# Reading v, k and q of one accumulator bank on ScalarE first, with VectorE's low halves behind

## The chip, the core and the metric

The kernel runs on one core of a Trainium2 chip. A core has TensorE (PE, matmuls; its weight loads are shown as PEld), VectorE (DVE), ScalarE (ACT), GpSimd (POOL) and SyncE (SP, which here issues nearly all DMAs). Each engine works through its own list of instructions in order, and engines wait for each other by semaphores. Matmul results land in PSUM, which has eight banks; ACT and DVE read them from there. The metric is the device time of one execution in microseconds; lower is better.

## The reference

One layer of a streaming encoder with two token mixers side by side: differential attention ("A", 4 heads of two rotated 64-wide queries and keys) and stick-breaking attention ("B", 8 heads, no rotation). There are 2048 prompt rows, and 8 x 16 sample rows with a cache of 512 keys each. Cut to what matters here:

```python
qa, ka, va, za, qb, kb, vb, zb, ga, gb = split(h @ w_in)
qa, ka = rope(qa, pos), rope(ka, pos)
# A
w = softmax(s1) - lam * softmax(s2);  oa = w @ va
# B: no rotation
z = qb @ kb.T * 64 ** -0.5;  mask = kpos < qpos
log_1m = where(mask, log_sigmoid(-z), 0)
log_a = log_sigmoid(z) + reverse_cumsum(log_1m) - log_1m
ob = where(mask, exp(log_a), 0) @ vb
y = (sigmoid(ga) * ya + sigmoid(gb) * yb) @ w_out
```

The new keys and values of both mixers are outputs as well.

## The kernel before

**Units and tiles.** The work of the mixers is cut into eight units, two heads' worth of 128 columns each; units 0, 2, 4 and 6 are of kind 0 (A) and 1, 3, 5 and 7 of kind 1 (B). Each unit goes over 17 row tiles of 128 rows, the sample tile first. A tile has a projection (`project`): 24 matmuls of 128 x 512 into one bank named ps_mm (L467), giving q, k, v and the gate input z, 128 columns each. Two banks serve ps_mm in turn. Beside it run 24 matmuls of the output gates (L543, bank ps_t). Six transposes (L561, L565) turn q and k, and copies (L575, L576) bring them to SBUF.

**Precision by halves.** Matmuls run in float16, so every operand is a pair: a high half, rounded to float16, and a low half, the remainder. ScalarE makes the high half (`S.activation`, L318 within `split`, and L501 for the query, which it writes twice), VectorE the low half (`V.scalar_tensor_tensor`, L323 and L502), which reads the same source and subtracts the high half.

**Leaving the bank.** `finish`, at the projection's last matmul, empties the bank. For kind 1: ACT copies k and v (pr, L485) and z (L489) out in float32, then come `halves(vt)`, `halves(k16)` and `query`, each a high half on ACT and then its low half on DVE. All of them read the one bank. For kind 0 the bank is read for pr (L481) and v only; q and k come from the rotated rows in SBUF that POOL makes (L508 to L513).

**Scores of B.** For each head and 512 keys: two matmuls and a mask into a bank ps_s (L708, L709, L712; three banks), two sigmoids on ACT (L134), a scan on DVE (L682). At the end of up to 1024 keys POOL multiplies (L688), ACT casts the high half (L616), DVE makes the low half (L619), and SP issues a transposing DMA (L626) whose result feeds the value matmuls (L769, L770; L765 to L767 for A).

**What sets the order.** The program is written as interleaved streams: scores of a tile, pieces of projections some 5 tiles ahead (`take`, `position`, `LEAD`), weights' preparation at the side. From that the framework's scheduler builds each engine's list by its own model of time and puts in the semaphores. Two engines never get the same PSUM bank at once: it orders their accesses, reads among themselves too. So the list of every engine can change around an edit. Projections reload their rows (hs, three tiles, L444) by DMA; a tile's hs is free when its projection and its gates are done.

Of the kernel before, what the change touches and what calls it, by code (L numbers as in the profile page):

```python
# [21 lines left out]
AF = mybir.ActivationFunctionType  # L22
ALU = mybir.AluOpType
# [3 lines left out]
P = 128  # L27
# [97 lines left out]
def layer_kernel(ctx: ExitStack, tc: tile.TileContext, a: dict):  # L125
    nc = tc.nc
    V, S, G, T = nc.vector, nc.scalar, nc.gpsimd, nc.tensor
# [12 lines left out]
    def kept(x):  # L140
        tc.keep_in_program_order(x)
        return x
# [37 lines left out]
    def out_rows(name, t, lo, n):  # L180
        p, s = outs[name]
        return p[t * P : (t + 1) * P, lo : lo + n] if t < NT else s[:, lo : lo + n]
# [28 lines left out]
    def bank(tag, dt=F32):  # L211
        return ps.tile([P, 512 if dt == F32 else 1024], dt, tag=tag, name=f"ps_{tag}", bufs=BANKS[tag])
# [102 lines left out]
    def split(hi, lo, src, s, on=None):  # L315

        if on is S:
            S.activation(out=hi, in_=src, func=AF.Identity, scale=s)  # L318
        elif on is G:
            G.tensor_scalar(out=hi, in0=src, scalar1=s, scalar2=0.0, op0=ALU.mult, op1=ALU.add)  # L320
        else:
            V.tensor_scalar(out=hi, in0=src, scalar1=s, scalar2=None, op0=ALU.mult)
        V.scalar_tensor_tensor(out=lo, in0=src, scalar=s, in1=hi, op0=ALU.mult, op1=ALU.subtract)  # L323
# [114 lines left out]
    def late(u, t):  # L438
        return u == 7 and NT - LATE <= t < NT

    def fetch_h(u, t):
        ahead[u, t] = hs[len(fetched) % 3].bitcast(F16).rearrange("p (f k n) -> p f k n", f=2, n=P)
        fetched.append(t)
        load(out=ahead[u, t], in_=hT_d[t // 4][:, t % 4, :, :, :])  # L444

    def project(U, t):

        kind, h, sc, sq = U["kind"], U["h"], U["sc"], U["sq"]
        g, i = t // 4, t % 4
        box = {}  # L450

        def start():
            if t in at_hand:
                box["h"] = at_hand.pop(t)
            else:
                if (U["u"], t) not in ahead:
                    fetch_h(U["u"], t)
                box["h"] = ahead.pop((U["u"], t))
            box["p"] = bank("mm")
            if kind == 0:  # L460
                box["r"] = stg.tile([P, 96], F32, tag="rope", name="rope")
                load(out=box["r"], in_=a["shapes"][:, t * 96 : t * 96 + 96])

        def mm(n):
            hi, wi = ((0, 0), (0, 1), (1, 0))[n % 3]
            k = n // 3
            T.matmul(box["p"], box["h"][:, hi, k, :], U["w"][k][:, wi, :], start=(n == 0), stop=(n == 3 * KT - 1))  # L467

        def piece(n):
            if n == 0:  # L470
                start()
            for j in range(2 * n, 2 * n + 2):
                mm(j)
            if n == 11:
                finish()

        def finish():
            p, s2, s = box["p"], sc[:, 2:3], sq[:, 0:1]
            pr = stg.tile([P, 512], F32, tag="pr", name="pr", bufs=3)
            if kind == 0:  # L480
                S.activation(out=pr, in_=p, func=AF.Identity, scale=sc[:, 1:2])  # L481
            elif t == NT:
                S.activation(out=pr[:, P:512], in_=p[:, P:512], func=AF.Identity, scale=sc[:, 1:2])
            else:
                S.activation(out=pr[:, P:384], in_=p[:, P:384], func=AF.Identity, scale=sc[:, 1:2])  # L485

                assert t % len(rings) not in silu_z
                silu_z[t % len(rings)] = rings[t % len(rings)]
                S.activation(out=rings[t % len(rings)], in_=p[:, 384:512], func=AF.Identity, scale=sc[:, 1:2])  # L489

            qb = qbuf[t % len(qbuf)]
            k16 = stg.tile([P, 2, 2, 64], F16, tag="k16", name="k16")
            vt = kvp.tile([P, 2, 2, 64], F16, tag="v", name="v", bufs=V_BUFS)

            def halves(dst, src, scale):
                src = src.rearrange("p (c d) -> p c d", d=64)
                split(dst[:, :, 0, :], dst[:, :, 1, :], src, scale, S)

            def query(src, scale):
                src = src.rearrange("p (c d) -> p c d", d=64)  # L500
                S.activation(out=qb[:, 0, :, :, :], in_=src.unsqueeze(2).to_broadcast([P, 2, 2, 64]), func=AF.Identity, scale=scale)  # L501
                V.scalar_tensor_tensor(out=qb[:, 1, :, 0, :], in0=src, scalar=scale, in1=qb[:, 0, :, 0, :], op0=ALU.mult, op1=ALU.subtract)  # L502
            if kind == 0:
                cosT, sinT = box["r"][:, 0:32], box["r"][:, 32:96]
                x4 = pr[:, 0:256].rearrange("p (c f d) -> p c f d", c=4, f=2)
                rot = stg.tile([P, 256], F32, tag="rot", name="rot")
                r2 = stg.tile([P, 256], F32, tag="r2", name="r2", bufs=1)
                G.tensor_tensor(out=rot.rearrange("p (c f d) -> p c f d", c=4, f=2), in0=x4,  # L508
                                in1=cosT.unsqueeze(1).unsqueeze(1).to_broadcast([P, 4, 2, 32]), op=ALU.mult)
                G.tensor_tensor(out=r2.rearrange("p (c f d) -> p c f d", c=4, f=2), in0=x4[:, :, ::-1, :],  # L510
                                in1=sinT.rearrange("p (f d) -> p f d", f=2).unsqueeze(1).to_broadcast([P, 4, 2, 32]),
                                op=ALU.mult)
                G.tensor_tensor(out=rot, in0=rot, in1=r2, op=ALU.add)  # L513
                halves(vt, p[:, 256:384], s2)
                query(rot[:, 0:128], s)
                halves(k16, rot[:, 128:256], s)
            else:
                rot = pr
                halves(vt, p[:, 256:384], s2)
                halves(k16, p[:, 128:256], s2)  # L520
                query(p[:, 0:128], s2)
            nk, nv = ("ak", "av") if kind == 0 else ("bk", "bv")
            load(out=out_rows(nk, t, h * P, P), in_=rot[:, 128:256])
            load(out=out_rows(nv, t, h * P, P), in_=pr[:, 256:384])
            ui = (h + 4 * kind) * P
            if kind == 0 or t == NT:
                load(out=z_d[t][:, ui : ui + P], in_=pr[:, 384:512])
            U["v"][t] = vt
            if t == NT:
                load(out=s_d[U["u"]][:, 6:8, :], in_=vt.rearrange("p c f d -> p c (f d)"))  # L530
            U["q16", t], U["k16", t] = qb, k16

        g0, gw = GATES[U["u"]]
        per = 1024 // gw if gw else 0

        def gate_piece(n):

            if n == 0:
                box["g"] = bank("t")
            for j in range(per * n, per * n + per):  # L540
                hi, wi = ((0, 0), (0, 1), (1, 0))[j % 3]
                k = j // 3
                x = T.matmul(box["g"][:, 0:gw], box["h"][:, hi, k, :], U["wg"][k // per][:, k % per, wi, :], start=(j == 0), stop=(j == 3 * KT - 1))  # L543
# [916 lines left out]
    with ExitStack() as c2:  # L1460
        def pool2(name, bufs):
            return c2.enter_context(tc.tile_pool(name=name, bufs=bufs, reuse_waits="tile"))
# [3 lines left out]
        s2 = pool2("s2", 2)  # L1466
# [169 lines left out]
```

## Time and profile before

| | us |
|---|---|
| timed runs | 2216.34, 2220.72, 2229.65 |
| median | 2220.72 |
| profiled execution | 2225.32 |
| its span, first to last instruction | 2223.5 |
| TensorE busy in the span | 2061.2 |
| VectorE busy | 1743.8 |
| ScalarE busy | 1606.2 |

The span falls into a start of some 120 us, then the units one after the other, A and B in turn up to about 1760 us, and the merge of the branches with the sample's attention behind that. An engine's idle time is put down to the instruction that released it; such a row gives total, number of waits and the longest. Idle time of an engine that isn't the slowest costs nothing by itself.

### The profile page before, as it was taken

What the parts mean: (1) busy time and instruction counts of PE and PEld (TensorE: products, weight loads), DVE (VectorE), ACT (ScalarE), POOL (GpSimd) and SP (SyncE); (2) the same over time, 40 slices, a digit from 0 to 9 for tenths busy, and PEclk for the clock granted to TensorE, in tenths of its full rate; (3) what the DMA queues carried; (4) which work ended last, traced back from release to release, by engine and by line L of the source; (5) the groups of instructions that cost most, each with busy time, mean ns of one, the idle gap of its engine ahead of it and who ended that gap; (6) DMA issues with size and microseconds to landing.
All of it is one profiled execution on the core that took longest, in us unless ns stands there. A gap on an engine that the chain in (4) does not pass through costs nothing. (4 is left out here: it accounts for less than half of the span.)

```text
span 2223.5 us, 41495 instructions
## 1 busy us (share of the span) xinstructions
PE 2061.2 (93%) x14608; PEld 1110.4 (50%) x14608; DVE 1743.8 (78%) x3799; ACT 1606.2 (72%) x3212; POOL 699.6 (31%) x608
## 2 busy tenths in 40 slices
PE   5999999999999999999999998989998788899997
PEld 3655555555555455555554554555454444444443
DVE  4667869789887788988778888777789877787864
ACT  3978677789877677978677788876688666666531
POOL 1232014356410443742024355301334412111210
PEclk8999999999999999999999999999999899999999
DMA  9778559899796889979879999985787999999762
GB/s 323 258 241 201 120 139 217 181 227 203 200 252 158 222 201 202 207 205 221 198 195 216 191 224 207 241 181 130 159 170 155 201 280 255 230 254 224 194 166 67
DMA packets 824978, 451.05 MB, mean 203 GB/s; under 512 B 556122, under 2 KB 763274, under 8 KB 824256
## 3 DMA queue, kind: packets, MB, share of 16 engines
q1 hardware_dynamic: 823820, 448.01, 82.7%
q8 instruction: 114, 1.87, 0.3%
q14 instruction: 96, 0.79, 0.1%
q10 hardware_dynamic: 948, 0.39, 0.1%
HBM read 229.87 MB, written 86.02 MB: 142 GB/s over the span
## 5 line engine op out<-in xcount | busy, mean ns | idle before, releaser
L688 POOL TENSOR_TENSOR sc_p<-sc_p,sc_n 128x127 f32<-128x127 f32 (+7 forms) x192 | 313.3, 1635 | 663.1 <-DVE sc_n L682 510.6
L467 PEld LDWEIGHTS <-hs 128*128 128x128 f16 x3120 | 293.3, 99 | 318.5 <-issue 6.4
L467 PE MATMUL ps_mm<-wa,hs 128*128 128x512 f16 x1590 | 391.2, 382 | 5.3 <-DMA hs<-hT_d 5.0
L467 PE MATMUL ps_mm<-wb,hs 128*128 128x512 f16 x1530 | 377.4, 380 | 0.0
L682 DVE TENSOR_TENSOR_SCAN sc_n<-ps_s,sc_n,zero_t 128x512 f32<-128x512 f32 x192 | 245.4, 1278 | 33.3 <-ACT ps_s L134 28.1
L708 PE MATMUL ps_s<-k,qst 128*128 128x512 f16 (+3 forms) x640 | 223.2, 350 | 30.0 <-DVE sc_n L682 22.8
L543 PEld LDWEIGHTS <-hs 128*128 128x128 f16 x1632 | 155.0, 98 | 181.7 <-DVE qst L576 5.1
L543 PE MATMUL ps_t<-wa,hs 128*128 128x512 f16 x1020 | 242.3, 380 | 2.1 <-DVE qst L576 2.0
L619 DVE TENSOR_TENSOR sc_n<-sc_p,sc_n 128x128 f16<-128x128 f32 (+7 forms) x192 | 217.7, 1137 | 32.9 <-ACT sc_n L616 32.3
L134 ACT ACTIVATE sc_p<-ps_s,usc 128x512 f32<-128x512 f32 (+3 forms) x320 | 203.9, 637 | 34.4 <-PE ps_s L709 23.0
L709 PE MATMUL ps_s<-k,qst 128*128 128x512 f16 (+3 forms) x640 | 223.6, 350 | 0.0
L616 ACT CAST sc_n<-sc_p 128x128 f16<-128x128 f32 (+7 forms) x192 | 155.0, 809 | 57.3 <-POOL sc_p L688 55.8
L134 ACT ACTIVATE ps_s<-ps_s,usc 128x512 f32<-128x512 f32 (+3 forms) x320 | 196.3, 613 | 0.0
L543 PE MATMUL ps_t<-wb,hs 128*128 128x512 f16 x612 | 151.7, 383 | 4.8 <-DMA hs<-hT_d 2.1
L769 PE MATMUL ps_o<-v,wt 128*128 128x128 f16 x1088 | 135.2, 224 | 22.1 <-DMA wt<-sc_n 21.9
L1535 PE MATMUL ps_o<-wo,wb 128*128 128x512 f16 x624 | 141.6, 382 | 1.1 <-ACT wb L1309 1.1
L602 DVE TENSOR_SCALAR_CACHE_REDUCE sc_p<-ps_s,usc 128x512 f32<-128x512 f32 (+3 forms) x160 | 106.2, 664 | 35.7 <-PE ps_s L709 20.5
L770 PE MATMUL ps_o<-v,wt 128*128 128x64 f16 x1088 | 127.1, 196 | 0.0
L769 PEld LDWEIGHTS <-wt 128*128 128x128 f16 x1088 | 101.0, 100 | 50.1 <-DMA wt<-sc_n 25.3
L682 DVE TENSOR_TENSOR_SCAN sc_n<-ps_s,zero_t 128x128 f32<-128x128 f32 (+3 forms) x128 | 104.0, 813 | 27.7 <-ACT ps_s L134 27.7
L1501 PEld LDWEIGHTS <-wa 128*128 128x128 f16 x816 | 77.7, 98 | 94.2 <-issue 4.1
L1544 POOL TENSOR_TENSOR x<-m,x 128x512 f32<-128x512 f32 x32 | 45.6, 1427 | 247.1 <-DVE m L1539 138.7
(378 smaller groups left out, 4548.6 us busy)
## 6 DMA issues: line engine op xcount, KB each, us to landing
hs<-hT_d SPq DMA_DIRECT2D x132, 512.0 KB
g_d<-gt SPq DMA_DIRECT2D x68, 256.0 KB
out_dram<-pr SPq DMA_DIRECT2D x204, 64.0 KB
o_d<-o SPq DMA_DIRECT2D x136, 64.0 KB
wa<-g_d SPq DMA_DIRECT2D x17, 512.0 KB
wb<-g_d SPq DMA_DIRECT2D x17, 512.0 KB
hs<-o_d SPq DMA_DIRECT2D x17, 512.0 KB
wide<-in_w_ada_dram SPq DMA_DIRECT2D x8, 1024.0 KB
```

The source lines that it names most:

```text
L134: i = S.activation(**kw)
L467: T.matmul(box["p"], box["h"][:, hi, k, :], U["w"][k][:, wi, :], start=(n == 0), stop=(n == 3 * KT - 1))
L543: x = T.matmul(box["g"][:, 0:gw], box["h"][:, hi, k, :], U["wg"][k // per][:, k % per, wi, :], start=(j == 0), stop=(j == 3 * KT - 1))
L616: x = S.copy(out=hi, in_=src)
L619: V.tensor_tensor(out=lo, in0=src, in1=hi, op=ALU.subtract)
L682: V.tensor_tensor_scan(out=dst[:, lo : lo + n][:, ::-1], data0=src[:, 0:n][:, ::-1], data1=zero_t[:, 0:1].to_broadcast([P, n]), initial=fi ...
L688: G.tensor_tensor(out=p[:, 0:m], in0=p[:, 0:m], in1=n[:, 1 : m + 1], op=ALU.mult)
L708: T.matmul(p[:, 0:n], qst[:, c, :], kk[:, c, 0:n], start=True, stop=False)
L709: T.matmul(p[:, 0:n], qst[:, 2 + c, :], kk[:, c, 0:n], start=False, stop=not diag)
L769: T.matmul(po[:, c * P : (c + 1) * P], wt[:, wj, :], vt[:, c, :, :], start=first, stop=False)
L770: T.matmul(po[:, c * P : c * P + 64], wt[:, nb + wj, :], vt[:, c, 0, :], start=False, stop=last)
L1535: T.matmul(po, st["y"][:, yi * 8 + k, :], wo[j * 4 + k // 2][:, wi, k % 2, :], start=(n == 0), stop=(n == 3 * KT - 1))
```

## The change

For kind 1 the three high halves are read first, then the three low halves follow. For kind 0 the order of the six instructions is what it was; the helpers are only split in two.

```diff
-            def halves(dst, src, scale):
-                src = src.rearrange("p (c d) -> p c d", d=64)
-                split(dst[:, :, 0, :], dst[:, :, 1, :], src, scale, S)
-
-            def query(src, scale):
-                ...
+            def parts(src):
+                return src.rearrange("p (c d) -> p c d", d=64)
+
+            def high(dst, src, scale):
+                S.activation(out=dst[:, :, 0, :], in_=parts(src), func=AF.Identity, scale=scale)
+
+            def low(dst, src, scale):
+                V.scalar_tensor_tensor(out=dst[:, :, 1, :], in0=parts(src), scalar=scale, in1=dst[:, :, 0, :], op0=ALU.mult, op1=ALU.subtract)
+
+            def query_high(src, scale):
+                S.activation(out=qb[:, 0, :, :, :], in_=parts(src).unsqueeze(2).to_broadcast([P, 2, 2, 64]), func=AF.Identity, scale=scale)
+
+            def query_low(src, scale):
+                V.scalar_tensor_tensor(out=qb[:, 1, :, 0, :], in0=parts(src), scalar=scale, in1=qb[:, 0, :, 0, :], op0=ALU.mult, op1=ALU.subtract)
...
             else:
                 rot = pr
-                halves(vt, p[:, 256:384], s2)
-                halves(k16, p[:, 128:256], s2)
-                query(p[:, 0:128], s2)
+                high(vt, p[:, 256:384], s2)
+                high(k16, p[:, 128:256], s2)
+                query_high(p[:, 0:128], s2)
+                low(vt, p[:, 256:384], s2)
+                low(k16, p[:, 128:256], s2)
+                query_low(p[:, 0:128], s2)
```

The number of instructions on each engine stays the same; lines behind L520 move by 12 (L616 is now L628, L682 is L694, L619 is L631, L749 is L761). On ACT, at the projection of tile 10 of unit 3, the list was this (pr, szs, v, k_10278 and qbuf are what the bank is read into, sc_p and sc_n the scores of B, ob an output of the value matmuls):

```order
L485 ACTIVATE pr<-ps_mm,usc_8232 128x256
L489 ACTIVATE szs<-ps_mm,usc_8232 128x128
L318 ACTIVATE v<-ps_mm,usc_8232 128x2x64
L134 ACTIVATE sc_p<-ps_s,usc_8232 128x512
L134 ACTIVATE ps_s<-ps_s,usc_8232 128x512
L134 ACTIVATE r_10317<-szs 128x128
L616 CAST sc_n<-sc_p 128x1024
L749 ACTIVATE ob<-ps_o,usc_8232 128x128
L318 ACTIVATE k_10278<-ps_mm,usc_8232 128x2x64
L616 CAST sc_n<-sc_p 128x128
```

There k stands six places behind v, and q (L501) four places behind k. At the same projection ACT's list with the change is:

```order
L134 ACTIVATE sc_p<-ps_s,usc_8232 128x512
L134 ACTIVATE ps_s<-ps_s,usc_8232 128x512
L134 ACTIVATE r_10317<-szs 128x128
L485 ACTIVATE pr<-ps_mm,usc_8232 128x256
L489 ACTIVATE szs<-ps_mm,usc_8232 128x128
L499 ACTIVATE v<-ps_mm,usc_8232 128x2x64
L499 ACTIVATE k_10278<-ps_mm,usc_8232 128x2x64
L505 ACTIVATE qbuf_213<-ps_mm,usc_8232 128x256
L761 ACTIVATE ob<-ps_o,usc_8232 128x128
L628 CAST sc_n<-sc_p 128x128
```

The five reads of the bank stand in one piece, and two sigmoids and the silu's sigmoid now stand ahead of it. On DVE, the low halves of the same projection stood here before (k and qst are the copies of the turned keys and queries, o an output of B):

```order
L576 COPY qst<-ps_t 128x512
L323 SCALAR_TENSOR_TENSOR v<-ps_mm,usc_8232,v 128x2x64
L682 SCALAR_TENSOR_TENSOR sc_n<-ps_s,sc_n,zero_t 128x512
L732 TENSOR_TENSOR szs<-szs,r_10317 128x128
L619 TENSOR_TENSOR sc_n<-sc_p,sc_n 128x1024
L750 SCALAR_TENSOR_TENSOR o<-ps_o,usc_8232,ob 128x128
L323 SCALAR_TENSOR_TENSOR k_10278<-ps_mm,usc_8232,k_10278 128x2x64
L619 TENSOR_TENSOR sc_n<-sc_p,sc_n 128x128
L682 SCALAR_TENSOR_TENSOR sc_n<-ps_s,zero_t 128x256
L502 SCALAR_TENSOR_TENSOR qbuf_213<-ps_mm,usc_8232,qbuf_213 128x2x64
```

With scans and other low halves between them, v, k and q lie nine places apart. DVE's list at this projection with the change is:

```order
L588 COPY qst<-ps_t 128x512
L694 SCALAR_TENSOR_TENSOR sc_n<-ps_s,sc_n,zero_t 128x512
L744 TENSOR_TENSOR szs<-szs,r_10317 128x128
L502 SCALAR_TENSOR_TENSOR v<-ps_mm,usc_8232,v 128x2x64
L502 SCALAR_TENSOR_TENSOR k_10278<-ps_mm,usc_8232,k_10278 128x2x64
L508 SCALAR_TENSOR_TENSOR qbuf_213<-ps_mm,usc_8232,qbuf_213 128x2x64
L762 SCALAR_TENSOR_TENSOR o<-ps_o,usc_8232,ob 128x128
L631 TENSOR_TENSOR sc_n<-sc_p,sc_n 128x128
L631 TENSOR_TENSOR sc_n<-sc_p,sc_n 128x1024
L694 SCALAR_TENSOR_TENSOR sc_n<-ps_s,zero_t 128x256
```

The three low halves stand together behind a scan, and the scan of 256 columns comes behind them.

More of the change, by code (lines that the diff above doesn't have):

```diff
@@ L493, in finish @@
             vt = kvp.tile([P, 2, 2, 64], F16, tag="v", name="v", bufs=V_BUFS)
-            def halves(dst, src, scale):
-                src = src.rearrange("p (c d) -> p c d", d=64)
-                split(dst[:, :, 0, :], dst[:, :, 1, :], src, scale, S)
-            def query(src, scale):
-                src = src.rearrange("p (c d) -> p c d", d=64)
-                S.activation(out=qb[:, 0, :, :, :], in_=src.unsqueeze(2).to_broadcast([P, 2, 2, 64]), func=AF.Identity, scale=scale)
-                V.scalar_tensor_tensor(out=qb[:, 1, :, 0, :], in0=src, scalar=scale, in1=qb[:, 0, :, 0, :], op0=ALU.mult, op1=ALU.subtract)
+            def parts(src):
[8 more added lines that the diff above has]
+                V.scalar_tensor_tensor(out=qb[:, 1, :, 0, :], in0=parts(src), scalar=scale, in1=qb[:, 0, :, 0, :], op0=ALU.mult, op1=ALU.subtract)
             if kind == 0:
@@ L513, in finish @@
                 G.tensor_tensor(out=rot, in0=rot, in1=r2, op=ALU.add)
-                halves(vt, p[:, 256:384], s2)
-                query(rot[:, 0:128], s)
-                halves(k16, rot[:, 128:256], s)
+                high(vt, p[:, 256:384], s2)
+                low(vt, p[:, 256:384], s2)
+                query_high(rot[:, 0:128], s)
+                query_low(rot[:, 0:128], s)
+                high(k16, rot[:, 128:256], s)
+                low(k16, rot[:, 128:256], s)
             else:
                 rot = pr
-                halves(vt, p[:, 256:384], s2)
-                halves(k16, p[:, 128:256], s2)
-                query(p[:, 0:128], s2)
+                high(vt, p[:, 256:384], s2)
+                high(k16, p[:, 128:256], s2)
+                query_high(p[:, 0:128], s2)
+                low(vt, p[:, 256:384], s2)
+                low(k16, p[:, 128:256], s2)
+                query_low(p[:, 0:128], s2)
             nk, nv = ("ak", "av") if kind == 0 else ("bk", "bv")
```

## The prediction

> **What bounds the kernel now.** I read the page first, then busy time by stretch, then the groups of the instructions that the change touches, then the waits. The page gives the span and the shares.
>
> ```profile
> span 2223.5 us, 41495 instructions
> PE 2061.2 (93%) x14608; PEld 1110.4 (50%) x14608; DVE 1743.8 (78%) x3799; ACT 1606.2 (72%) x3212; POOL 699.6 (31%) x608
> ```
>
> The profiled execution took 2225.32 us, of which the span is 2223.5 and 1.8 lies around it; the three timed runs have the median 2220.72. I work differences out in the trace and take them off the median.
>
> TensorE is busy 93% of the time. The change acts only where projections of stick-breaking units run, which is four stretches, since projections run some tiles ahead of the scores that use them. The columns are stretch, length, then busy time of PE, PEld, DVE, ACT and POOL, the granted clock, the DMA share and GB/s:
>
> ```profile
> 215.00:420.00 205.00, 197.41 (x1386) 107.78 (x1384) 163.90 (x361) 150.54 (x331) 46.72 (x44) 0.99 0.69 162
> 660.00:860.00 200.00, 191.83 (x1324) 103.49 (x1323) 156.76 (x312) 149.21 (x314) 60.01 (x53) 1.00 0.82 196
> 1090.00:1290.00 200.00, 192.13 (x1323) 103.12 (x1322) 158.30 (x296) 152.23 (x320) 68.14 (x58) 1.00 0.85 194
> 1500.00:1700.00 200.00, 187.84 (x1341) 102.36 (x1339) 158.33 (x294) 144.88 (x304) 62.91 (x51) 0.97 0.71 155
> ```
>
> TensorE is idle 7.6, 8.2, 7.9 and 12.2 us there, 35.8 us in 805. That is all that a better order of ACT and DVE could win in these stretches while TensorE's own work is unchanged.
>
> One place looks different, the end of the last unit:
>
> ```profile
> 1670.00:1680.00 10.00, 9.75 (x88) 5.64 (x86) 9.74 (x15) 10.00 (x22) 3.76 (x4) 1.00 0.68 156
> 1690.00:1700.00 10.00, 6.83 (x37) 3.75 (x37) 9.89 (x13) 6.26 (x12) 4.77 (x3) 0.57 0.74 145
> 1700.00:1710.00 10.00, 7.19 (x63) 3.97 (x61) 9.89 (x10) 7.94 (x13) 4.92 (x4) 1.00 0.61 119
> ```
>
> Here DVE is busy 9.7 to 9.9 us of every 10 while TensorE falls to 7: VectorE's scans set the pace, and what arrives late at DVE is lost.
>
> **The change, part by part.** It removes waits of ScalarE and adds no instruction. The groups concerned (busy, mean ns | idle before, and what ended it):
>
> ```profile
> L318 ACT ACTIVATE k<-ps_mm,usc 128x128 f16<-128x128 f32 x68 | 25.7, 378 | 24.6 <-DVE v L323 24.2 <-PE ps_t L561 0.2
> L501 ACT ACTIVATE qbuf<-ps_mm,usc 128x256 f16<-128x256 f32 x68 | 32.2, 474 | 41.9 <-DVE k L323 41.9
> L323 DVE SCALAR_TENSOR_TENSOR v<-ps_mm,usc,v 128x128 f16<-128x128 f32 x136 | 46.6, 342 | 16.0 <-ACT v L318 15.2
> L323 DVE SCALAR_TENSOR_TENSOR k<-ps_mm,usc,k 128x128 f16<-128x128 f32 x68 | 22.8, 336 | 1.5 <-ACT k L318 1.5
> L502 DVE SCALAR_TENSOR_TENSOR qbuf<-ps_mm,usc,qbuf 128x128 f16<-128x128 f32 x68 | 23.2, 341 | 13.6 <-ACT qbuf L501 13.2
> ```
>
> ACT stands 24.2 + 41.9 = 66.1 us, about 1 us for each of the 68 projections, until DVE has finished a low half, although k's and q's high halves need nothing from it: the two engines take turns on the bank. DVE stands 1.5 + 13.2 = 14.7 us for k and q, and up to 15.2 us for v (rotated units share that row). All of this is replaced by one hand-over per projection.
>
> What one projection looks like (unit 3, tile 10, that of the order rows shown above):
>
> ```profile
> 802.30 0.52 ACT L485 ACTIVATE pr<-ps_mm,usc 128x256 f32<-128x256 f32 x1
> 802.65 0.42 ACT L489 ACTIVATE szs<-ps_mm,usc 128x128 f32<-128x128 f32 x1
> 802.90 0.42 ACT L318 ACTIVATE v<-ps_mm,usc 128x128 f16<-128x128 f32 x1
> 804.84 0.34 DVE L323 SCALAR_TENSOR_TENSOR v<-ps_mm,usc,v 128x128 f16<-128x128 f32 x1
> 805.85 0.36 ACT L318 ACTIVATE k<-ps_mm,usc 128x128 f16<-128x128 f32 x1
> 806.10 0.29 ACT L616 CAST sc_n<-sc_p 128x128 f16<-128x128 f32 x1
> 807.87 0.34 DVE L323 SCALAR_TENSOR_TENSOR k<-ps_mm,usc,k 128x128 f16<-128x128 f32 x1
> 808.24 0.47 ACT L501 ACTIVATE qbuf<-ps_mm,usc 128x256 f16<-128x256 f32 x1 [0.24 <-DVE k L323]
> 810.22 0.32 DVE L502 SCALAR_TENSOR_TENSOR qbuf<-ps_mm,usc,qbuf 128x128 f16<-128x128 f32 x1
> ```
>
> The bank is read from 802.30 to 810.54, 8.2 us, because each turn also queues behind whatever its engine has in order. With the reads together, ACT's five starts lie 0.35, 0.25, 0.25 and 0.25 apart (802.30 to 802.65 to 802.90, and 805.85 to 806.10 for a read of 128 columns), and q takes 0.47: 1.6 us in one piece. Three lows follow, each start some 0.26 behind the other, 0.9 us. The bank could be free after 2.5 us instead of 8.2.
>
> Does anyone need it earlier? Hardly. TensorE's waits near it in the whole span (total, times, longest):
>
> ```profile
> PE ps_mm L467 <- DVE v L323: 0.5, 2, 0.3
> PE ps_s L708 <- DVE sc_n L682: 22.8, 25, 2.2
> PE ps_mm L467 <- DMA hs<-hT_d: 5.0, 1, 5.0
> PE ps_o L769 <- DMA wt<-sc_n: 21.9, 11, 4.2
> ```
>
> The next projection waited for a bank 0.5 us in all: that gain is nil, covered by the second bank. What ACT and DVE can still do for TensorE is to hand back score banks (22.8 us, 25 waits) and to bring the weights earlier to the transposing DMA (21.9 us, 11 waits).
>
> Gain, tail. Between 1600 and 1690 us the waits were:
>
> ```profile
> DVE sc_n L682 <- ACT ps_s L134: 12.0, 15, 2.2
> ACT k L318 <- DVE v L323: 2.1, 2, 1.7
> ACT qbuf L501 <- DVE k L323: 1.6, 2, 1.3
> ```
>
> ACT loses 2.1 + 1.6 = 3.7 us there, DVE waits 12.0 us for its sigmoids, and both are nearly full at 1670. Bounds 0 and 3.7; I take 3, since DVE is the pace there.
>
> Gain, the three earlier stretches. TensorE's idle is 7.6 + 8.2 + 7.9 = 23.7 us. Bounds: nothing, because the waits removed were ACT's and TensorE was working meanwhile, and all of it. I take a quarter, 6 us: most of this idle has releasers that the change doesn't touch.
>
> Loss. The sigmoids that stood between v and k or k and q now wait behind two more reads, 0.25 + 0.25 = 0.5 us, and scans queue behind two more low halves, again about 0.5 us. Were each of 64 tiles to pass 0.5 us on to TensorE, it would be 32 us. But TensorE waited for a scan 25 times at 640 score chunks, 4%, as this row's count and idle say:
>
> ```profile
> L708 PE MATMUL ps_s<-k,qst 128*128 128x512 f16 (+3 forms) x640 | 223.2, 350 | 30.0 <-DVE sc_n L682 22.8 <-DVE sc_n L602 4.9 <-DVE csc L951 1.4
> L682 DVE TENSOR_TENSOR_SCAN sc_n<-ps_s,sc_n,zero_t 128x512 f32<-128x512 f32 x192 | 245.4, 1278 | 33.3 <-ACT ps_s L134 28.1
> ```
>
> so I take 2 us, bounds 0 and 32. SP's and POOL's work keeps its instructions; the output of k and v comes from pr, which is read first as before.
>
> Sum: -3 - 6 + 2 = **-7 us**, so 2223.5 goes to about 2216.5 in a profiled span, and the median to **2214 us**, 0.3% faster. A measurement of this kernel tells about 0.5% (11 us) from no change, so my forecast is "no difference that can be told".
>
> **The rivals.**
>
> Rival A, the blocks hurt (slower). Place: ACT's five reads and DVE's three lows in one piece, ahead of sigmoids and scans, with three score banks. Price as above, 0.5 us a tile at most; with 0.35 us for each of 64 tiles it is 22 us, less nothing won: 2243 us. It decides from (11 + 9) / 64 = 0.3 us a tile if the gains come, 0.17 if they don't. For it: 25 waits for scans exist already, up to 2.2 us. Against: the 66.1 us that ACT gets back are more than the 0.5 x 64 = 32 us that it delays.
>
> Rival B, another order around it (slower). The scheduler places all instructions anew. In the first stick-breaking unit the gates' matmuls slip behind the projections: counted in the two orders, 216 gate matmuls stood ahead of the end of tile 8's projection, and now 168. A tile of hs is freed by its gates, so its reload starts later, and the same re-dealing moves the weights' transposes on SP's queue. The nearest rows:
>
> ```profile
> 1465.73 0.29 PE L765 MATMUL ps_o<-v,wt 128*128 128x128 f16 x1 [5.61 <-DMA wt<-sc_n]
> 1465.00:1475.00 10.00, 8.32 (x57) 5.37 (x58) 5.59 (x15) 3.98 (x8) 0.00 (x0) 0.75 0.63 199
> ```
>
> One late transfer cost 5.6 us, and the 10 us after it ran at a clock of 0.75, 2.5 us more. Three such stalls are 24 us: 2220.7 - 7 + 24 = 2238 us. Against: TensorE has work of other tiles between, and it met the hs wait once in the span. [...]
>
> Rival C, more than I count (faster). If ACT's 66.1 us was what kept DVE and TensorE late all along, half of the 35.8 us of idle goes, 18 us: 2203 us. For it: DVE waited 28.1 us for the sigmoids ahead of long scans. Against: ACT is busy only 150 of 205 us in these stretches, so it had room to catch up.
>
> Rival D, the change isn't what it says. The order says it is, nearly: v, k and q stand together on ACT in 58 of 68 projections, and the three lows together on DVE in 62; 2 and 1 before. Its time is 2220 us, and its chance goes into the forecast's.
>
> **How the numbers follow.** Forecast (with D) 0.45, C 0.28, A 0.15, B 0.12. The forecast's own range is 2207 to 2224. Of it, 0.04 lies under 2210 (faster) and nothing over 2232; A and B give slower 0.27. So faster 0.32, same 0.41, slower 0.27. The range over the cases reaches to C's 2203 with some 5 us below it, and to between B and A: 2198 to 2240, with a tenth left out on either side.
>
> **What would show it.** Right: ACT's waits of k and q for DVE lows gone (66 us to a few), one wait of a few tenths at v's low, the bank held about 3 us, TensorE's idle in the four stretches down by some 6 us, the tail up to 1770 us done about 3 us sooner within the unit. Rival A: the score matmul's wait for scans well over 22.8 us. Rival B: single TensorE waits of 4 us or more for hs or wt, and clock under 0.95 behind them. Rival C: idle near 18 us. The forecast is wrong if TensorE's busy time itself moves, or if the time changes in stretches without such projections, as in the merge after 1770 us.

## The result, and the profile after

The changed kernel takes 2231.11 us (median of 14 runs, 2226.32 to 2237.99), beside 2222.35 us for the kernel before on the same chip (14 runs). The ratio is 1.0036, with a 95% interval of 1.0025 to 1.0047: 0.36% or 8 us slower. That is less than the 0.5% taken as the bound of "no difference", but it is beyond its own interval, and on the other side of the forecast of 2214 us. The profiled execution took 2230.99 us. The page begins:

```profile
span 2229.2 us, 41523 instructions
PE 2071.2 (93%) x14608; PEld 1115.3 (50%) x14608; DVE 1740.6 (78%) x3799; ACT 1602.8 (72%) x3212; POOL 714.1 (32%) x608
```

TensorE's idle time is 2229.2 - 2071.2 = 158.0 us, 4 less than the 162.3 of before. The span grew all the same, because the same 14608 matmuls were busy 10 us longer; the mean granted clock fell from 0.980 to 0.974. This pair of traces makes the clock's part too large: the 14 timed runs of the changed kernel have a mean clock of 0.976, and 35 runs of the kernel before, taken with the first experiments, 0.977. How the loss divides into idle and slower time can't be told from one trace of each.

**The intended part came.** The groups of the reads and lows (busy, mean ns | idle before, and what ended it):

```profile
L499 ACT ACTIVATE k<-ps_mm,usc 128x128 f16<-128x128 f32 x68 | 26.5, 389 | 3.5 <-PE ps_t L573 3.5
L505 ACT ACTIVATE qbuf<-ps_mm,usc 128x256 f16<-128x256 f32 x68 | 34.0, 501 | 0.0
L502 DVE SCALAR_TENSOR_TENSOR v<-ps_mm,usc,v 128x128 f16<-128x128 f32 x136 | 46.7, 344 | 21.1 <-ACT v L499 11.4 <-ACT qbuf L505 9.1
L508 DVE SCALAR_TENSOR_TENSOR qbuf<-ps_mm,usc,qbuf 128x128 f16<-128x128 f32 x68 | 23.1, 340 | 0.0
```

ACT no longer waits for a low half: the 66.1 us are gone, and one hand-over is left at v's low, 9.1 / 68 = 0.13 us a projection. At tile 10 of unit 3 ACT's timeline shows the block of reads, from the first to the last:

```profile
813.03 0.47 ACT L485 ACTIVATE pr<-ps_mm,usc 128x256 f32<-128x256 f32 x1
...
814.14 0.51 ACT L505 ACTIVATE qbuf<-ps_mm,usc 128x256 f16<-128x256 f32 x1
```

and DVE's the lows behind it:

```profile
814.86 0.34 DVE L502 SCALAR_TENSOR_TENSOR v<-ps_mm,usc,v 128x128 f16<-128x128 f32 x1
...
815.38 0.34 DVE L508 SCALAR_TENSOR_TENSOR qbuf<-ps_mm,usc,qbuf 128x128 f16<-128x128 f32 x1
```

At this projection the bank is held from 813.03 to 815.72, 2.7 us where it was 8.2. But ACT's waits went elsewhere, to TensorE (waits of ACT, before):

```profile
ACT sc_p L134 <- PE ps_s L709: 23.0, 35, 2.8
ACT gt L548 <- PE ps_t L543: 19.9, 15, 5.7
```

and after:

```profile
ACT sc_p L134 <- PE ps_s L721: 45.2, 48, 4.8
ACT gt L560 <- PE ps_t L555: 34.9, 22, 6.3
```

These two rows alone rose by 37.2 us. A good part of the time that ACT was given it spends waiting for TensorE.

**Where the time went.** The same instructions stand in both traces, so their starts can be laid side by side (starts from the timelines; last column the lead of before):

| place | before | after | difference |
|---|---|---|---|
| unit 1 begins: first pr of unit 1 (ACT) | 220.4 | 220.4 | 0 |
| unit 1 ends: first output of unit 2 (ACT) | 554.1 | 560.0 | +5.9 |
| sixth gate copy of unit 7 (ACT) | 1562.1 | 1566.3 | +4.2 |
| eighth gate copy of unit 7 (ACT) | 1590.7 | 1588.4 | -2.3 |
| last scan of B (DVE) | 1750.2 | 1759.1 | +8.9 |
| end of the span | 2223.5 | 2229.2 | +5.7 |

Three places carry most of it: unit 1 loses 5.9, unit 7 wins 6.5 within two tiles, and the way from there to the last scan loses 11.2. The long way between unit 1 and unit 7 gives back 1.7, and the merge behind the last scan 3.2. Each column is one execution, so a difference of 1 or 2 us says little.

**Unit 1.** Busy time by 20 us from 340 us on, before and then after (columns as in the prediction):

```profile
340.00:360.00 20.00, 19.90 (x135) 10.44 (x132) 17.17 (x32) 14.14 (x32) 9.07 (x9) 1.00 1.00 236
360.00:380.00 20.00, 18.72 (x127) 9.90 (x125) 17.96 (x32) 15.05 (x29) 9.22 (x7) 1.00 0.92 218
```

```profile
340.00:360.00 20.00, 16.83 (x103) 8.58 (x101) 15.04 (x33) 11.03 (x25) 7.21 (x7) 0.91 0.66 159
360.00:380.00 20.00, 17.04 (x99) 8.38 (x98) 16.84 (x24) 10.94 (x22) 9.40 (x8) 0.91 0.61 170
```

By these rows TensorE does 202 matmuls instead of 262 in the 40 us. The timeline of the changed kernel's TensorE has the two stalls:

```profile
353.33 0.23 PE L781 MATMUL ps_o<-v,wt 128*128 128x128 f16 x1 [3.15 <-DMA wt<-sc_n]
373.20 6.18 PE L467 MATMUL ps_mm<-wb,hs 128*128 128x512 f16 x20 [2.96 <-DMA hs<-hT_d]
```

Both are transfers: turned weights that aren't there yet, and rows (hs) whose tile is free only when its gates are done, and these now stand further behind the projections (the prediction counted 168 of them in place of 216). That the late gates make the rows late is read from the lists; the pins below test it.

**Unit 7** wins at the only long hs wait that before had in a projection. Before, in TensorE's timeline:

```profile
1568.94 4.41 PE L467 MATMUL ps_mm<-wa,hs 128*128 128x512 f16 x12 [5.02 <-DMA hs<-hT_d]
```

In the changed kernel TensorE's waits between 1555 and 1600 us are two, and that one isn't among them:

```profile
PE ps_t L555 <- DVE qst L588: 2.0, 1, 2.0
PE ps_t L573 <- ACT gt L560: 1.7, 1, 1.7
```

**The entry of the merge.** Before, TensorE's timeline has the last score chunk (L708) ahead of the last late gates (L543):

```profile
1745.99 0.38 PE L708 MATMUL ps_s<-k,qst 128*128 128x512 f16 x1 [0.52 <-DVE sc_n L682]
1747.38 1.47 PE L543 MATMUL ps_t<-wb,hs 128*128 128x512 f16 x6 [0.80 <-DMA hs<-hT_d]
```

After, one chunk (L720) stands behind them, and behind their wait for hs:

```profile
1750.45 2.74 PE L555 MATMUL ps_t<-wb,hs 128*128 128x512 f16 x6 [2.05 <-DMA hs<-hT_d]
...
1757.01 0.38 PE L720 MATMUL ps_s<-k,qst 128*128 128x512 f16 x1
...
1769.51 0.29 PE L781 MATMUL ps_o<-v,wt 128*128 128x128 f16 x1 [5.66 <-DMA wt<-sc_n]
```

The first six of these gate matmuls take 2.74 us at a clock of 0.50 (the last section has the windows), where six took 1.47 before at 1.00. The chunk's scan starts at 1759.08, POOL, ACT, DVE and the transposing DMA follow it, and TensorE stands 5.66 us for its weights. Of 1760 to 1770 us it is busy 1.81, beside 7.83 before (the row is of the changed kernel):

```profile
1760.00:1770.00 10.00, 1.81 (x32) 1.45 (x30) 4.60 (x16) 6.25 (x8) 2.89 (x2) 0.67 0.73 153
```

So the theory to be tested (T1): reading the high parts first is worth about nothing, and the time comes from places in the engines' lists that the scheduler dealt anew around the edit. Its rival (T2): the blocks of reads and lows cost by themselves, tile by tile.

### The profile page after: what moved, and what is told of

Same layout as the page of the kernel before. It is cut to its first block, busy times and chain, and to the rows that moved or that the text cites. A ratio compares the mean times of both kernels' runs of the same rounds, so it can differ in the third digit from the quotient of the medians.

```text
span 2229.2 us, 41523 instructions
## 1 busy us (share of the span) xinstructions
PE 2071.2 (93%) x14608; PEld 1115.3 (50%) x14608; DVE 1740.6 (78%) x3799; ACT 1602.8 (72%) x3212; POOL 714.1 (32%) x608
## 4 chain that ended last, share of the span: by engine, by line
PE 24%; DVE 9%; DMA 9%; ACT 5%; issue 3%; POOL 2%; SPq 0%; DVEq 0%; POOLq 0%; ACTq 0%
PE ps_mm L467 5%; PE ps_t L555 5%; PE ps_o L1547 4%; PE ps_mm L1513 3%; DMA wt<-sc_n 2%; DMA hs<-o_d 2%; DVE sc_n L694 2%; PE ps_s L720 1%; PE ps_s L721 1%; DMA hs<-hT_d 1%; POOL sc_p L700 1%; ACT sc_p L134 1%; PE ps_o L781 1%; DVE sc_n L631 1%; DMA x<-in_w_out_dram 1%
## 5 line engine op out<-in xcount | busy, mean ns | idle before, releaser
L700 POOL TENSOR_TENSOR sc_p<-sc_p,sc_n 128x127 f32<-128x127 f32 (+7 forms) x192 | 318.9, 1664 | 667.9 <-DVE sc_n L694 507.4
L694 DVE TENSOR_TENSOR_SCAN sc_n<-ps_s,sc_n,zero_t 128x512 f32<-128x512 f32 x192 | 245.5, 1279 | 43.9 <-ACT ps_s L134 38.0
L555 PEld LDWEIGHTS <-hs 128*128 128x128 f16 x1632 | 156.6, 99 | 194.4 <-DVE qst L588 11.2
L720 PE MATMUL ps_s<-k,qst 128*128 128x512 f16 (+3 forms) x640 | 222.6, 349 | 28.4 <-DVE sc_n L694 22.2
L631 DVE TENSOR_TENSOR sc_n<-sc_p,sc_n 128x128 f16<-128x128 f32 (+7 forms) x192 | 217.4, 1136 | 31.0 <-ACT sc_n L628 30.4
L628 ACT CAST sc_n<-sc_p 128x128 f16<-128x128 f32 (+7 forms) x192 | 156.2, 819 | 66.4 <-POOL sc_p L700 66.0
L781 PE MATMUL ps_o<-v,wt 128*128 128x128 f16 x1088 | 130.2, 222 | 27.2 <-DMA wt<-sc_n 27.0
L514 POOL TENSOR_TENSOR rot<-pr,rope 128x256 f32<-128x256 f32 x68 | 58.6, 862 | 206.5 <-ACT pr L481 134.4
L694 DVE TENSOR_TENSOR_SCAN sc_n<-ps_s,zero_t 128x128 f32<-128x128 f32 (+3 forms) x128 | 104.1, 814 | 25.7 <-ACT ps_s L134 25.6
```

The lines of the kernel that those rows point to most:

```text
L628: x = S.copy(out=hi, in_=src)
L631: V.tensor_tensor(out=lo, in0=src, in1=hi, op=ALU.subtract)
L694: V.tensor_tensor_scan(out=dst[:, lo : lo + n][:, ::-1], data0=src[:, 0:n][:, ::-1], data1=zero_t[:, 0:1].to_broadcast([P, n]), initial=fi ...
L700: G.tensor_tensor(out=p[:, 0:m], in0=p[:, 0:m], in1=n[:, 1 : m + 1], op=ALU.mult)
L720: T.matmul(p[:, 0:n], qst[:, c, :], kk[:, c, 0:n], start=True, stop=False)
L781: T.matmul(po[:, c * P : (c + 1) * P], wt[:, wj, :], vt[:, c, :, :], start=first, stop=False)
```

## The experiments

All ratios are to the kernel before, run on the same chip beside them, with 12 timed executions each (6 in the sixth and eighth, 10 in the twelfth) and 95% intervals.

**Which units carry it.** The first three take the new order in some units only (here unit 1):

```diff
             else:
                 rot = pr
-                high(vt, p[:, 256:384], s2)
-                high(k16, p[:, 128:256], s2)
-                query_high(p[:, 0:128], s2)
-                low(vt, p[:, 256:384], s2)
...
+                if U["u"] in (1,):
+                    high(vt, p[:, 256:384], s2)
+                    high(k16, p[:, 128:256], s2)
+                    query_high(p[:, 0:128], s2)
...
+                else:
+                    high(vt, p[:, 256:384], s2)
+                    low(vt, p[:, 256:384], s2)
+                    high(k16, p[:, 128:256], s2)
...
```

> High halves first in unit 1 alone; units 3, 5 and 7 keep turns on the bank, and their lists and the merge's are those of before. The changed kernel is 0.36% (8 us) slower than before. Theory 1 (another order, places): the loss sits in two places, unit 1, where gates slip behind projections and hs is reloaded late, and the entry of the merge. Then this run has unit 1's share: +5 to +6 us over before (+0.25%), with single waits of TensorE of about 3 us for hs and wt between 340 and 560 us. Theory 2 (five reads and three lows in one piece delay sigmoids and scans in every tile, the same in each unit): a quarter of the 8 us, +2 us.

Unit 1 alone: 2230.34 us, ratio 1.0026 (1.0011 to 1.0042), which is 5.8 us slower. Its first output of unit 2 starts at 564.6 us, 10.5 later than before. The time is T1's; of the two waits that T1 named, that for wt came larger (up to 5.2 us) and that for hs smaller (up to 1.5 us).

> High halves first in units 3, 5 and 7, unit 1 keeps turns. Theory 1: without unit 1's late reload, with the merge's entry as in the changed kernel: +2 to +4 us over before. Theory 2: three quarters of the loss, +6 us.

Units 3, 5 and 7: 2227.66 us, 1.0008 (0.9993 to 1.0024). That is 1.8 us, within the noise and just under T1's 2 to 4; T2's 6 us lies outside.

> High halves first in units 3 and 5 alone, where the order of TensorE hardly changes; unit 1, unit 7 and the merge stand as before. Theory 1: no loss, 0 to -2 us against before (the aligned traces show -1.5 and +1 us for these units). Theory 2: half of the loss, +4 us.

Units 3 and 5: 2223.63 us, 0.9999 (0.9985 to 1.0013). Half of the block reads neither win nor lose anything that can be measured: the interval goes from -3.3 to +2.9 us, T2's +4 lies outside, and so do the 4 us of gain that the prediction put on these two stretches (a quarter of 16.1 us). The first two kernels' losses, 5.8 and 1.8 us, make up 7.6 of the change's 8, though each is known to some 3 us only.

**The merge's entry, first reading.** In the changed kernel the scale of the cached values (L243, waiting 2.52 us for TensorE) stands ahead of the last scan on DVE, and behind it before. This edit puts it behind:

```diff
-        V.tensor_scalar(out=q, in0=square, scalar1=2.0 ** -46, scalar2=None, op0=ALU.max)
+        first = V.tensor_scalar(out=q, in0=square, scalar1=2.0 ** -46, scalar2=None, op0=ALU.max)
+        if behind is not None:
+            tc.add_manual_dep(first.ins, behind.ins.name, NOSYNC, reason="behind the last scan")
...
-        vs = scales(total(add_up_all(csums), 8), res, "s_c", 8)
+        vs = scales(total(add_up_all(csums), 8), res, "s_c", 8, behind=last_scan[0])
```

> The changed kernel, but the scale of the cached values (VectorE, out of ps_t) may not stand ahead of the last scan of unit 7 in VectorE's list; it is pinned behind it. In the changed kernel VectorE waited 2.5 us for that scale's matmul with the last scan behind it, and TensorE then waited 5.7 us for the last weights. Theory 1: 4 to 6 us faster than the changed kernel, so +2 to +4 us over before, and the 5.7 us wait gone. Theory 2: no change against the changed kernel, +8 us.

2231.14 us, 1.0033 (1.0018 to 1.0047): nothing won. The scale did move, but the scan did not come sooner, as its row in DVE's timeline says:

```profile
1758.30 1.28 DVE L698 TENSOR_TENSOR_SCAN sc_n<-ps_s,sc_n,zero_t 128x512 f32<-128x512 f32 x1 [3.19 <-ACT ps_s L134]
```

It waits for the sigmoid, and that for the score chunk. The scale had stood in time that was idle anyway, so this reading was wrong, and the row points to TensorE's list.

**The merge's entry, second reading.** The last twelve pieces of late gates are held back until the last tile's scores are written:

```diff
                 k = -(-len(behind) * LATE_SHARE[m] // sum(LATE_SHARE[m:]))
+                if m == -1:
+                    k, held = len(behind) - 12, behind[-12:]
                 pieces += [(1.0, fn) for fn in behind[:k]]
...
         give(interleaved(pieces, qk, side), (PIECE, CHUNK, 0.0))
+        if n == len(steps) - 1:
+            give([(0, 1.0, fn) for fn in held], (PIECE,))
+            behind.clear()
```

> The changed kernel, but the last tile's scores are written ahead of the last group of late gates, so TensorE does the last score chunk first, as before, instead of behind 24 gate matmuls that wait 2 us for their rows. Theory 1 (order, two places): the last scan some 9 us earlier, TensorE's 5.7 us wait for the last weights at most 4, and 3 to 5 us faster than the changed kernel, +3 to +5 us over before. If the merge's entry costs nothing: no change, +8.

2228.39 us, 1.0015 (1.0002 to 1.0028). In TensorE's timeline the last chunk stands ahead of the gates' wait again:

```profile
1747.80 0.38 PE L720 MATMUL ps_s<-k,qst 128*128 128x512 f16 x1
1751.79 2.52 PE L555 MATMUL ps_t<-wb,hs 128*128 128x512 f16 x6 [2.72 <-DMA hs<-hT_d]
```

The wait for hs is there still, and longer (2.72 us), but no score stands behind it. The last scan starts at 1752.7 us instead of 1759.1 (T1 had 9 us earlier, it is 6.4), and TensorE's longest wait for the last weights falls from 5.7 to 1.6 us. The gain on the changed kernel, 1.0036 to 1.0015, is within T1's 3 to 5 us.

**Unit 1, first attempt.** The first matmul of each of unit 1's projections keeps its place in the order in which the program is written, so that gates written ahead of it stay ahead:

```diff
-            T.matmul(box["p"], box["h"][:, hi, k, :], U["w"][k][:, wi, :], start=(n == 0), stop=(n == 3 * KT - 1))
+            x = T.matmul(box["p"], box["h"][:, hi, k, :], U["w"][k][:, wi, :], start=(n == 0), stop=(n == 3 * KT - 1))
+            if U["u"] == 1 and t < NT and n == 0:
+                kept(x)
```

> The changed kernel, high halves first in all four units, but in unit 1 a projection's first matmul is pinned behind what the program writes ahead of it, the gates of the tile before included. Theory 1: the gates no longer slip, waits for hs (3.0 us) and most of those for wt (8.1 us) in unit 1 go, 4 to 6 us faster than the changed kernel, +2 to +4 us over before. If unit 1's loss comes from the reads themselves: no change, +8.

2232.72 us, 1.0041 (1.0028 to 1.0053). With the hold of the late gates as well:

> Both pins together, the change itself untouched. Theory 1: the loss is undone, -2 to +1 us against before. Theory 2 (the reads in one piece cost time): still +4 or more.

2229.66 us, 1.0032 (1.0019 to 1.0045). Both missed T1's numbers. The trace of the first says why it settles nothing (ACT's timeline, then busy time):

```profile
264.16 0.47 ACT L487 ACTIVATE pr<-ps_mm,usc 128x256 f32<-128x256 f32 x1 [1.60 <-PE ps_mm L467]
```

```profile
220.00:300.00 80.00, 70.89 (x504) 40.24 (x504) 56.84 (x151) 46.94 (x105) 0.00 (x0) 0.96 0.57 113
340.00:360.00 20.00, 17.67 (x136) 10.90 (x134) 16.45 (x44) 13.29 (x31) 7.61 (x7) 0.91 0.80 227
360.00:380.00 20.00, 20.00 (x137) 10.60 (x135) 18.05 (x31) 16.97 (x37) 9.61 (x9) 1.00 0.91 229
```

From 340 to 380 us TensorE is busy 37.7 us, beside 33.9 in the changed kernel and 38.6 before: most of the hole is filled. But the pin also forbade the first projection to run early: its first read starts at 264 us instead of 220, and TensorE is busy 70.9 of the 80 us from 220 on, beside 77.8 in the changed kernel:

```profile
220.00:300.00 80.00, 77.80 (x575) 43.78 (x573) 61.58 (x168) 55.33 (x123) 0.00 (x0) 1.00 0.56 119
```

The edit took away one hole and dug another: its first output of unit 2 starts at 565.6 us, later than the changed kernel's 560.0.

**An edit with nothing to win by itself.** The kernel before, with its turns, but with the query ahead of k:

```diff
-                halves(k16, p[:, 128:256], s2)
                 query(p[:, 0:128], s2)
+                halves(k16, p[:, 128:256], s2)
```

> The kernel before with turns on the bank, k and q merely swapped (q's turn ahead of k's). The edit has nothing to win or lose by itself, but the scheduler places the lists anew; in them, as in the changed kernel, one score chunk stands behind the last gates, and gates slip by a tile in four tiles of unit 1. Theory 1: a loss of 2 to 5 us over before without any change of the turns. Theory 2: 0 us.

2231.51 us, 1.0033 (1.0021 to 1.0046). The reads in turns, two of them swapped, cost as much as the change did, 7.3 us where T1 had 2 to 5. In TensorE's list one chunk of scores has again come to stand behind the last gates, and the trace shows it:

```profile
1753.93 2.74 PE L543 MATMUL ps_t<-wb,hs 128*128 128x512 f16 x6 [2.03 <-DMA hs<-hT_d]
...
1760.72 0.38 PE L708 MATMUL ps_s<-k,qst 128*128 128x512 f16 x1
```

Unit 1 loses nothing here (the table below has 333.8 us, and 333.7 for before), so whatever gates slipped there had no price.

**Both places put back.** The pin from tile 4 of unit 1 on (`t >= 4 and t < NT`), where the gates start to slip, so that the first projections run as early as they did, and the hold:

> The changed kernel with two orders put back: in unit 1 from tile 4 on, the projection may not be traced ahead of the gates it used to follow (the earlier pin from tile 0 had moved unit 1's first projection from 220 to 264 us and so brought a loss of its own), and the last 12 late-gate pieces are held until the last tile's scores are traced. T1 (the loss comes from the re-dealt places in unit 1 and at the merge's entry): TensorE's busy time in 340 to 380 us goes from 33.9 to 37.5 or more, TensorE's waits for wt and hs in unit 1 from 11 us to under 5, the first product with v of unit 2 starts at 554 to 557 us again (changed kernel: 560), and the ratio to before is 0.999 to 1.001 (2222 to 2226 us). T2 (the blocks of reads themselves cost in unit 1): the hole between 340 and 380 us stays, ratio 1.0015 as with the hold alone (2228 us).

2222.14 us, 0.9985 (0.9971 to 0.9999): faster than before by 0.15%, just beyond the interval, and faster than the changed kernel. T1 had 0.999 to 1.001, so it came out lower than either theory said. In the same 40 us of unit 1:

```profile
340.00:360.00 20.00, 20.00 (x142) 10.95 (x140) 16.57 (x30) 15.64 (x32) 7.72 (x8) 1.00 0.73 180
360.00:380.00 20.00, 20.00 (x131) 10.32 (x130) 18.25 (x29) 16.74 (x35) 10.02 (x9) 1.00 0.79 198
```

No idle at all, and the clock at 1.00. TensorE's waits for wt and hs from 215 to 570 us went from 8.1 + 0.2 + 3.0 us to 3.7 + 0.5 + 0, and the first output of unit 2 starts at 551.1 us (560.0 in the changed kernel, 554 to 557 expected).

> High parts first in units 3, 5 and 7 alone, and the last 12 late-gate pieces held as before. T1: unit 1 is as in the kernel before, the merge's entry is mended, so the 4 us that the hold gave the changed kernel come off 2227.7: 2221 to 2225 us, ratio 0.998 to 1.0003; below 0.999 would be a version that beats both. T2 (the hold helps only in company of unit 1's order): 2227 us, ratio 1.0008.

2222.29 us, 0.9985 (0.9972 to 0.9997). Unit 1 as before, and the hold: also faster than both, as T1 said.

> The kernel before with the hold and nothing else (its scores already stand ahead of the last gates). T1 (the hold mends a misplacement that the kernel before does not have): within 2 us of before, ratio 0.999 to 1.001. Rival T3 (the hold is a gain of its own, whatever the order): 4 us faster, ratio 0.998, and then its gain in the changed kernel says nothing about the changed order.

2225.70 us, 1.0002 (0.9988 to 1.0016). The hold wins nothing where no chunk was misplaced, so T3 falls.

> The kernel before with query ahead of k (turns kept), and the hold. T1 (the swap lost its 7 us mostly at the merge's entry, where one chunk of scores stands behind the last gates as in the changed kernel): 4 to 6 us come back, 2225 to 2228 us, ratio 1.0005 to 1.0015. T2 (the swap lost them by q being read before k): 2231 us, ratio 1.003.

2234.81 us, 1.0043 (1.0025 to 1.0061). This missed: the hold did put the chunk in its place and brought the last scan 3.4 us forward (1762.8 to 1759.4), but the trace was 3 to 5 us behind the first swap's from unit 3 on, the merge's start (VectorE's first reading of a merge product) came no sooner (1783.4 beside 1782.4), and the timed runs show nothing won. The time is nearer the one that T2 named, q being read before k. Against T2 stands that the swap loses nothing in unit 1 in either trace. It does lose some 4 us between 1060 and 1190 us in both: TensorE waits 3.6 us there, once, for a cached-key scale of VectorE's (csc, L951), where it waited 0.8 before. What the rest of its loss is was not settled, and neither is why the hold won nothing here.

**The places over all traces.** Three steps can be read in each kernel: unit 1, from its first copy pr to the first output of unit 2; unit 7, from its sixth to its eighth gate copy; and from there to the last scan.

| kernel | high first in unit 1 | in unit 7 | a chunk behind the last gates | unit 1, us | sixth to eighth, us | eighth to last scan, us |
|---|---|---|---|---|---|---|
| before | no | no | no | 333.7 | 28.6 | 159.5 |
| before, hold | no | no | no | 332.3 | 30.1 | 160.5 |
| units 3 and 5 | no | no | no | 335.7 | 28.9 | 161.9 |
| swap, hold | no | no | no | 334.7 | 28.9 | 161.0 |
| swap | no | no | yes | 333.8 | 29.2 | 168.6 |
| unit 1 alone | yes | no | no | 343.6 | 28.5 | 159.8 |
| units 3, 5, 7 | no | yes | yes | 334.4 | 21.0 | 172.6 |
| units 3, 5, 7, hold | no | yes | no | 331.8 | 20.5 | 164.4 |
| after | yes | yes | yes | 339.6 | 22.2 | 170.6 |
| after, scale behind scan | yes | yes | yes | 341.5 | 22.1 | 171.9 |
| after, hold | yes | yes | no | 340.0 | 20.5 | 164.7 |
| after, pin from tile 0 | pinned | yes | yes | starts late | 22.2 | 170.3 |
| after, pin from tile 0, hold | pinned | yes | no | starts late | 20.5 | 163.0 |
| after, pin from tile 4, hold | pinned | yes | no | 332.5 | 20.5 | 163.3 |

Every kernel with the new order in unit 1 and no pin takes 339.6 us or more there, and every kernel with turns or with the pin from tile 4 takes 332 to 336. Every kernel with the new order in unit 7 wins 6 to 10 us in the second step. They pay some 3 us of that back in the third (163.0 to 164.7 us beside 159.5 to 161.9, all without the chunk). The chunk costs 6 to 10 us in the third step, with either order in unit 7. About half of that is made up behind the last scan, where the five kernels with the chunk take 470 us on the mean and the nine others 474; that, and the 3 us of the new order, is how 11 us in the table of places go with the 4 to 5 us that the hold won in the timed runs.

## Why the prediction was wrong

**The step that failed.** The sum was -3 - 6 + 2, and it priced the new lists at nothing, with the words "SP's and POOL's work keeps its instructions". The lists were the result: unit 1 lost some 6 us and the chunk behind the last gates some 4 to 5 in the timed runs, and with both orders put back the same reads run 0.15% faster than before instead of 0.36% slower. The two gains of the sum weren't there either, as follows term by term.

**The waits removed.** Right in size: 66.1 us of ACT's waits gone, 0.13 us a projection left at v's low, the bank held 2.7 us for 2.5 forecast. The step that they buy TensorE nothing directly was argued ("TensorE was working meanwhile") and then not followed, since a part of its idle was booked as a gain all the same.

**The gain in the three earlier stretches, -6 us.** This term was wrong. TensorE's idle there, by the same four windows:

```profile
215.00:420.00 205.00, 195.27 (x1368) 106.37 (x1366) 159.22 (x355) 145.84 (x325) 47.07 (x42) 0.98 0.67 155
660.00:860.00 200.00, 192.96 (x1321) 105.88 (x1320) 155.17 (x317) 145.31 (x311) 58.00 (x51) 0.98 0.81 195
1090.00:1290.00 200.00, 192.24 (x1309) 103.82 (x1307) 156.72 (x298) 149.14 (x315) 65.93 (x56) 0.99 0.82 189
1500.00:1700.00 200.00, 190.26 (x1358) 103.41 (x1356) 157.81 (x301) 146.35 (x310) 62.59 (x51) 0.98 0.71 154
```

It is 9.7, 7.0, 7.8 and 9.7 us, 34.3 in all and 1.5 less than before. The stretch of unit 1 got 2 us worse and that of unit 7 2.5 us better. Units 3 and 5 alone gave 0.9999. The fraction of a quarter had no row behind it; that these waits buy TensorE about nothing was the lower bound, and it was the right one.

**The gain at the tail, -3 us.** It was booked for DVE's scans getting their sigmoids sooner. Unit 7 did win 6.5 us, but by the loss of a 5.02 us wait of TensorE for hs, which the prediction's own fence showed as the one hs wait of a projection and did not count as something a new order could remove. Behind that the tail itself, without the chunk, takes some 3 us longer with the new order, where the prediction had it 3 us shorter; what makes it longer wasn't looked into. The chunk then cost more than the gain.

**The loss by blocks, 2 us, and Rival A.** TensorE's waits for scans are 22.2 us in 21 (22.8 in 25 before):

```profile
PE ps_s L720 <- DVE sc_n L694: 22.2, 21, 2.0
PE ps_o L781 <- DMA wt<-sc_n: 27.0, 10, 5.7
```

The term of 2 us was nearer nothing, and Rival A falls by this row and by units 3 and 5.

**Rival B, put at 0.12, is what happened**, as two events instead of three of 8 us. Its first place was right: gates behind projections in unit 1, a late hs (2.96 us), late weights (3.15 us), a clock under 0.95 behind them (0.91 in the two windows of 20 us). Its second, the entry of the merge, it did not name, though the two orders show it: the last group of gates had no score chunk behind it before, and one with the change. What counts is the place of an instruction in its list, not that the instructions stay the same, and only one place was looked for. The argument against B ("TensorE has work of other tiles between") did not hold at the merge's entry, since TensorE took its list in order: the chunk behind the gates whose hs wait of 2.05 us ended at 1750.45 started at 1757.01 us.

**Two readings on the clock.** The prediction took a move of TensorE's busy time as a sign of being wrong. It moved by 10 us, but that sign is weak: the kernel before with the hold, as fast as before, was profiled with 2073.6 us busy at a clock of 0.974. And the prediction's sign of Rival B was a lower clock behind waits of 4 us or more; it was 0.50 behind waits of 3.15 and 2.96 us and around one of 2.05 us, as the last section shows.

**Luck.** The stated range reached to 2240 us, so it holds the measured 2231, but by the rivals and not by the forecast. And the versions with the orders put back come near the forecast's sign for another reason than the one given: unit 7 runs without its hs wait in them, as the table shows.

**Shown and not shown.** The hold and the pin together, on the changed kernel, went from 1.0036 over 1.0015 to 0.9985, so the two places carry the whole loss. Unit 1's part has one more witness, the unit column above; the hold's has a counter-witness, the swap, where it put the chunk in its place and won nothing. That the new order in unit 7 removes the hs wait is shown by eight kernels that have the order, none of which has the wait, and six that don't, which have it at 4.2 to 5.4 us; that the freed bank and not another shift of the list does it isn't shown. In unit 1 the pin removed the hs wait and about half of the wt waits together, so their shares are not told apart. That the pin from tile 0 failed by the delayed first projection is read from its trace, and only supported by the pin from tile 4.

## What to carry to other kernels

Where a scheduler builds the engines' lists, an edit's price is that of the new lists: put the old and new order side by side on the busiest engine at every place where a transfer was just in time, and at the seam to the next phase, before any saved wait is counted. An edit of the same lines that should do nothing (here a swap that cost 0.33%, though not all of that was traced to places) gives a measure of what such a re-dealing can be worth, and a pin or hold that restores one place tells which part of the loss belongs to it. Waits of an engine that is not the bound, 66 us here, can go without the span getting shorter.

## What the runs showed of the hardware

The two waits of about 3 us in unit 1 were followed by a lower clock, and the one of 2.05 us at the merge's entry had it too. Windows of 1 us in the changed kernel, behind the wait of 3.15 us that ended at 353.33, behind that of 2.96 us that ended at 373.20, and around that of 2.05 us that ended at 1750.45, shortly behind one of 0.46 us (columns as in the prediction; the granted clock is the third number from the end):

```profile
353.00:354.00 1.00, 0.67 (x10) 0.67 (x11) 0.16 (x1) 0.00 (x0) 0.00 (x0) 0.90 0.54 127
355.00:356.00 1.00, 0.98 (x3) 0.13 (x2) 1.00 (x5) 0.45 (x2) 0.56 (x1) 0.50 0.62 242
357.00:358.00 1.00, 1.00 (x5) 0.44 (x4) 1.00 (x4) 1.00 (x4) 1.00 (x1) 0.90 0.00 0
374.00:375.00 1.00, 1.00 (x5) 0.40 (x3) 1.00 (x2) 0.69 (x2) 0.00 (x0) 0.64 1.03 418
377.00:378.00 1.00, 1.00 (x5) 0.33 (x4) 1.00 (x2) 0.00 (x0) 0.68 (x1) 0.66 0.00 0
1749.00:1750.00 1.00, 0.00 (x0) 0.00 (x0) 1.00 (x1) 1.00 (x4) 1.00 (x1) 0.92 0.42 168
1753.00:1754.00 1.00, 1.00 (x6) 0.44 (x5) 1.00 (x2) 0.44 (x1) 1.00 (x2) 0.87 0.00 0
```

Between the rows of each wait the clock is 0.50. In windows of 0.2 us it is 0.98 from 353.6 and 0.50 from 353.8, and 0.50 from 357.0 and 0.99 from 357.2. The other two places have one window between 1.00 and 0.50 at each step too. So it stepped here, and the means give the times of the steps: 353.8 to 357.2, 374.3 to 377.7 and 1749.8 to 1753.3, 3.4 us each time. In unit 1 the clock falls just behind the wait, at the last gates within it. Half of 3.4 us, some 1.7 us, is an estimate of what each adds where TensorE has work, and TensorE counts as busy in it; the six gate matmuls behind the third wait took 2.74 us, and 1.47 before. So part of the time that these three places took stands as busy and not as idle. The two of unit 1 make 3.4 of the 10 us by which the busy time rose; the rest wasn't followed wait by wait. Three places give no rule for the length of wait that goes with a lower clock: behind a wait of 2.06 us for weights that ended at 1364.95 in the same trace it is 1.00 in every window of 1 us from 1364 to 1370.
